# Attention scores of a head pair from 64 array rows each, in a PSUM bank each, with forget bias and mask added on VectorE

## The chip, the core and the metric

The program runs on one NeuronCore of a Trainium2 chip. Five engines work side by side, each through its own queue in order: TensorE (PE, matmuls into PSUM, with PEld for its weight loads), VectorE (DVE), ScalarE (ACT), GpSimd (POOL) and SyncE (SP), which here issues the weight loads. The metric is the device time of one execution in microseconds (us), the median of several runs.

## The reference

Two layers of a macaron block on 256 tokens of width 1024. The change lies in the forgetting attention of 8 heads of width 64; everything else (two SwiGLU blocks, a convolution branch, gates, a final gate) stays.

```
c  = cumsum(log_sigmoid(f_logit))                       # per head, over the tokens
for blk in 0, 1:                                        # blocks of 128 queries; keys up to the block's end
    sc = q[blk] @ k[:end].T * scale                     # (128 queries, 128 or 256 keys), contracted over 64
    sc = sc + (c[query] - c[key])                       # forget bias
    sc = where(query >= key, sc, -inf)
    pr = softmax(sc)
    out[blk] = pr @ v[:end]
```

In a softmax over the keys c[query] is the same for a whole row and drops out; only -c[key] matters.

## The kernel before, in words

Activations are kept transposed (`hT`, 128 features by 256 tokens per chunk). Each projection is done as three single-pass matmuls of split operands: `hi` and `lo` parts of the weights (`whi` made on ACT, `wlo` on DVE, lines 402 to 419) against `hi` and `lo` parts of the activations. Scores, transposes and probabilities times values stay plain fp32 matmuls, which the profile shows as two records each.

The order on PE, DVE and ACT is decided when the program is built. `Flow` (line 114) keeps a clock per engine; work is written as generators that yield (engine, planned cost, function) and waits on events or slots. `product` (line 258) puts the large projections on PE one after another, and lets the small operations of the generators in between whenever their planned time has come. DVE and ACT take the ready operation with the lowest `prio`; weight splits are fillers (`Weights.prio`, line 372), and the taps of the convolution (`taps`, line 919) have priority 4, so they fill what DVE has left. On the chip each engine then runs its list strictly in that order and waits where an input is late.

In `mixer` (line 898) the pieces that matter here follow one another on PE: the projections for the convolution and the values, the queries and keys (`heads`, line 1052), four gate blocks of 48 matmuls (line 1168), two blocks of 24 for `w_attn_out` (line 1191), two of 24 for `w_conv_out` (line 1217). The attention of four head pairs (`attention(j)`, line 1106) is slipped in between the gate matmuls.

Queries and keys lie in `QA` and `KA` with 66 rows per head: 64 features, and two rows that make the matmul add the forget bias (a row of ones against `ncum`, the negated running sum, and `cum` against ones). Each bank that `heads` fills holds four heads, the odd ones on partitions 64 to 127, so `heads_out` (line 1065) copies it in two halves to partitions 0 to 63. The 32 bias rows of both layers come by small DMAs from `forget` (line 994, DMAs at lines 1018 and 1019).

`softmax` (line 1079) runs once per pair and query block: two score matmuls into one bank of `xps` (two banks in all), a third matmul that adds the mask (`identb` against `later`, 256 columns of bf16), one DVE maximum over both heads, then per head an exponential on ACT that reads PSUM and sums, a reciprocal, and a scaling on ACT. Afterwards `attention` transposes the probabilities and multiplies by the values, each head into its own 64 partitions of one bank (line 1142).

The convolution ends with `conv_end` (line 1030): after the last tap ACT squares `acc` into `csq`, DVE adds it up, and PE sums over partitions (`xps<-ones,csq`). The chain goes on to `cs`, which the `w_conv_out` matmuls need.

Of the kernel before, what the change touches and what calls it, by code (L numbers as in the profile page):

```python
# [8 lines left out]
F32 = mybir.dt.float32  # L9
F32R = mybir.dt.float32r  # L10
I32 = mybir.dt.int32
BF16 = mybir.dt.bfloat16
AF = mybir.ActivationFunctionType
ALU = mybir.AluOpType
AX = mybir.AxisListType
PSUM = bass.MemoryType.PSUM

P = 128
T = 256
TT = T // P  # L20
D = 1024
KD = D // P
L = 2
H = 8
DH = 64
AW = H * DH
CC = 512
KC = CC // P
# [11 lines left out]
NEG = -3.0e38  # L40
# [19 lines left out]
PE, V, A = "pe", "vector", "scalar"  # L60


def vc(n, ptr=0):

    return 68 + 1.04 * n + 61 * ptr
# [6 lines left out]
class Event:  # L72
    at = None
# [10 lines left out]
class Slots:  # L84
# [6 lines left out]
    def ready(self):  # L91
        n = self.given - self.cap
        return 0 if n < 0 else self.ends.get(n)

    def take(self):
        self.given += 1
        return Handle(self, self.given - 1, self.make())


class Op:  # L100
# [13 lines left out]
class Flow:  # L114
# [9 lines left out]
    def spawn(self, gen, at=None, prio=1, lat=LAT):  # L124
        self.seq += 1
        c = Chain(gen, prio, lat, self.seq)
        self.resume(c, self.t[PE] if at is None else at, None)
        return c.ev
# [308 lines left out]
def trunk(ctx: ExitStack, tc: tile.TileContext, x, p, g_ff1, w_ff1_in, w_ff1_out, g_mix, w_in, b_f,  # L437
          w_attn_out, conv_w, conv_b, g_conv, w_conv_out, w_out, g_ff2, w_ff2_in, w_ff2_out,
          g_ple, w_ple_gate, w_ple_proj, g_final, out):
    nc = tc.nc  # L440
    tensor, vector, scalar = (Pinned(tc, e) for e in (nc.tensor, nc.vector, nc.scalar))
    flow = Flow()
    spawn, product = flow.spawn, flow.product
    pool = lambda **k: ctx.enter_context(tc.tile_pool(**k))
    const = pool(name="const", bufs=1)
# [5 lines left out]
    work = pool(name="work", bufs=2)  # L451
    small = pool(name="small", bufs=2)
    ps_mm = pool(name="ps_mm", bufs=6, space=PSUM)
    ps_x = pool(name="ps_x", bufs=2, space=PSUM)
    su_cm = tc.tile_pool(name="setup", bufs=1)
    su = su_cm.__enter__()
# [5 lines left out]
    xps = slots(2, ps_x, [P, 512], "xps")  # L462
# [3 lines left out]

    ident = const.tile([P, P], F32, name="ident")
    make_identity(nc, ident)

    identb = const.tile([P, P], BF16, name="identb")  # L470
    nc.gpsimd.tensor_copy(out=identb, in_=ident)
    later = const.tile([P, P], BF16, name="later")
    nc.gpsimd.memset(later, 0.0)
    nc.gpsimd.affine_select(out=later, in_=later, pattern=[[-1, P]], compare_op=ALU.is_ge, fill=NEG, base=0, channel_multiplier=1)
    ones = const.tile([P, P], F32, name="ones")
    vector.memset(ones, 1.0)
    by_token = const.tile([P, LINE], F32, name="by_token")
# [103 lines left out]
    def chunks(bank):  # L581
        return bank.t.rearrange("p (m t) -> p m t", m=2)
# [103 lines left out]
    class Norm:  # L686
        split_sum = False

        def __init__(self, gname, l):
            self.gname, self.l = gname, l  # L690
            self.xs = self.sum = self.got = None
            self.ready = [Event() for _ in range(KD)]
            self.tok, self.all, self.summed = Event(), Event(), Event()
# [114 lines left out]
    def bc(r, n, rows=P):  # L808
        return r.unsqueeze(1).to_broadcast([rows, n, T])
# [88 lines left out]
    def mixer(l, norm, nxt):  # L898
        W = w_in[l]
        norm.root()  # L900
        with tc.tile_pool(name="mixer", bufs=1) as ph, tc.tile_pool(name="attn", bufs=2) as at:
            QA = ph.tile([DH + 2, H, T], F32, name="QA")
            KA = ph.tile([DH + 2, H, T], F32, name="KA")
            abuf = ph.tile([P, KC, TAPS - 1 + T], F32, name="abuf")
            nc.gpsimd.memset(QA[DH:DH + 2], 1.0)
            nc.gpsimd.memset(KA[DH:DH + 2], 1.0)
            nc.gpsimd.memset(abuf[:, :, :TAPS - 1], 0.0)
            acc = ph.tile([P, KC, T], F32, name="acc")
            t1s, t2s = slots(2, at, [P, 512], "t1"), slots(2, at, [P, 512], "t2")
# [54 lines left out]
            in0 = spawn(conv_in(banks, (0, 1)))  # L964
# [29 lines left out]
            def forget():  # L994
                fl = at.tile([H, T], F32, name="fl", bufs=1)
                fe = at.tile([H, T], F32, name="fe", bufs=1)
                ncum = at.tile([H, T], F32, name="fc", bufs=1)
                bf = bf_t[:, l:l + 1]
                yield have_f8
                xp = yield xps  # L1000

                def go():
                    for tt in range(TT):
                        tensor.transpose(out=xp.t[:H, tt * P:(tt + 1) * P], in_=f8[:, tt], identity=ident)
                yield PE, 215, go

                yield A, ac(T), lambda: scalar.activation(out=fe, in_=xp.t[:H, :T], func=AF.Abs, bias=bf)
                yield A, ac(T) + 1283, lambda: scalar.activation(out=fe, in_=fe, func=AF.Exp, scale=-1.0)
                yield [(A, ac(T) + 1283, lambda: scalar.activation(out=fe, in_=fe, func=AF.Ln, bias=1.0)),
                       (V, vc(T), lambda: vector.tensor_scalar(out=fl, in0=xp.t[:H, :T], scalar1=bf, scalar2=0.0, op0=ALU.add, op1=ALU.min))]  # L1010
                xp.free()
                yield V, vc(T), lambda: vector.tensor_tensor(out=fl, in0=fl, in1=fe, op=ALU.subtract)
                cum = at.tile([H, T], F32, name="fe", bufs=1)
                oneb = ones[:H, 0:1].to_broadcast([H, T])
                yield V, vc(T), lambda: vector.tensor_tensor_scan(out=cum, data0=oneb, data1=fl, initial=0.0, op0=ALU.mult, op1=ALU.add)
                yield A, ac(T), lambda: scalar.activation(out=ncum, in_=cum, func=AF.Copy, scale=-1.0)
                for h in range(H):
                    nc.gpsimd.dma_start(out=QA[DH:DH + 1, h, :], in_=cum[h:h + 1, :])
                    nc.gpsimd.dma_start(out=KA[DH + 1:DH + 2, h, :], in_=ncum[h:h + 1, :])
                have_f.at = flow.now + 8000  # L1020
            spawn(forget(), prio=2)

            banks = block_a(W, norm.xs, KD, (C0 + 2 * P, C0 + CC + 2 * P), norm.ready)
# [28 lines left out]
            def heads(c0, dst, scale):  # L1052
                evs = []
                for mm in range(AW // (2 * P)):
                    bank = flow.take(mms)
                    blk = wts.take(W, 0, KD, c0 + mm * 2 * P, 2 * P)
                    for m in range(2):
                        for h in blk.halves:
                            ks = range(h.a, h.b)
                            piece(mm_b, MB, items_b(blk, bank, m, 0, ks, KD, norm.xs), [norm.ready[k] for k in ks])  # L1060
                    wts.release(blk)
                    evs.append(spawn(heads_out(bank, dst[:DH, 4 * mm:4 * mm + 4], scale)))
                return evs

            def heads_out(bank, dst, scale):
                yield norm.all
                for odd in range(2):
                    part, rows = dst[:, odd::2], slice(odd * DH, (odd + 1) * DH)
                    yield V, vc(2 * T), lambda: vector.scalar_tensor_tensor(out=part, in0=chunks(bank)[rows], scalar=scale,
                                                                            in1=bc(norm.rall[rows], 2, DH), op0=ALU.mult, op1=ALU.mult)  # L1070
                bank.free()

            have_qk = heads(Q0, QA, DH ** -0.5) + heads(K0, KA, 1.0)
# [2 lines left out]
            sms = slots(2, at, [P, TT, 2], "sm")  # L1076
            pTs = slots(1, at, [P, 6 * P], "pT")

            def softmax(h0, qb, sch, sm):

                sc, kl = sch.t, (qb + 1) * P
                xp = yield xps
                pt = xp.t.rearrange("p (h k) -> p h k", h=2)

                def go():
                    for i in range(2):
                        tensor.matmul(out=pt[:, i, :kl], lhsT=QA[:, h0 + i, qb * P:(qb + 1) * P], rhs=KA[:, h0 + i, :kl],
                                      start=i == 0, stop=False)
                    tensor.matmul(out=pt[:, :, qb * P:kl], lhsT=identb, rhs=later.unsqueeze(1).to_broadcast([P, 2, P]), start=False, stop=True)
                yield PE, 110 + 430 * (qb + 1), go  # L1090
                nm = small.tile([P, 2], F32, name=f"nm{qb}")
                yield V, vc(2 * kl), lambda: vector.tensor_reduce(out=nm, in_=pt[:, :, :kl], axis=AX.X, op=ALU.max, negate=True)

                def exps():
                    for i in range(2):
                        scalar.activation(out=sc[:, i], in_=pt[:, i, :kl], func=AF.Exp, bias=nm[:, i:i + 1], accum_out=sm[:, qb, i:i + 1])
                yield A, 2 * (ac(kl, 1) + 60), exps
                xp.free()
                yield V, vc(2), lambda: vector.reciprocal(out=sm[:, qb], in_=sm[:, qb])

                def norms():
                    for i in range(2):
                        scalar.activation(out=sc[:, i], in_=sc[:, i], func=AF.Copy, scale=sm[:, qb, i:i + 1])
                yield A, 2 * ac(kl, 1), norms

            def attention(j):
# [7 lines left out]
                    h = yield scs[qb]  # L1114
                    sch.append(h)
                sm = yield sms
                evs = [spawn(softmax(h0, qb, sch[qb], sm.t), at=flow.now) for qb in range(TT)]
                for e in evs:
                    yield e
                exp_done[j].at = flow.now  # L1120
# [289 lines left out]
```

## Time and profile before

| | |
|---|---|
| median of three runs | 1128.93 us (1128.48 to 1129.02) |
| profiled execution, device time | 1128.9 us |
| its span, first to last instruction | 1126.9 us |
| busy: PE, DVE, ACT, POOL | 1113.1, 833.3, 600.2, 30.5 us |
| granted TensorE clock | 0.998 of full speed |

The span is what the profile's instructions cover; about 2 us lie around it. A time "at 252.16" is counted from the span's start. A matmul's duration includes its way through the array and overlaps the next one's, so the cost of a matmul is read from start to start. Both layers run the same program; what layer 0 does at 252 us, layer 1 does at 804.7 us.

### The profile page before, as it was taken

How to read it: one execution, taken by the hardware profiler on the slowest of the kernel's cores; microseconds unless marked ns; L12 is line 12 of the kernel's file. 1: busy time of each engine (PE TensorE's matmuls, PEld its weight loads, DVE VectorE, ACT ScalarE, POOL GpSimd, SP SyncE). 2: the span in 40 equal slices, each digit the busy share in tenths (PEclk: the TensorE clock that was granted, in tenths of full speed). 3: DMA queues.
4: the chain of work that ended last, by engine and by line, in shares of the span. 5: the costliest groups of instructions: out<-in, count | busy, mean ns of one | idle time of the engine just before them, and what ended most of it. 6: DMA issues, size and time to landing. Idle time of an engine off the chain costs nothing.

```text
span 1126.9 us, 21344 instructions
## 1 busy us (share of the span) xinstructions
PE 1113.1 (99%) x8916; PEld 1069.8 (95%) x8916; DVE 833.3 (74%) x1256; ACT 600.2 (53%) x874; POOL 30.5 (3%) x58
## 2 busy tenths in 40 slices
PE   8999999999999999999999999999999999999997
PEld 8999999897789999999999999999877999999996
DVE  7766666899986867656896665569999787675665
ACT  6544445648555544444654444456566555444454
POOL 2000001020000000000000000012000000000000
PEclk9999999999999999999999999999999999999999
DMA  9655566454547565566466555664534656655541
GB/s 307 223 187 187 176 199 190 148 188 133 167 153 244 193 206 187 174 206 200 146 205 230 187 179 187 197 196 143 187 113 152 213 191 221 205 183 185 194 150 39
DMA packets 189665, 207.70 MB, mean 184 GB/s; under 512 B 5000, under 2 KB 174048, under 8 KB 189568
## 3 DMA queue, kind: packets, MB, share of 16 engines
q1 hardware_dynamic: 188064, 205.60, 55.7%
q8 instruction: 70, 1.15, 0.4%
q0 software_dynamic: 1472, 0.72, 0.3%
q14 instruction: 27, 0.22, 0.1%
q10 hardware_dynamic: 32, 0.01, 0.0%
HBM read 205.23 MB, written 1.05 MB: 183 GB/s over the span
## 4 chain that ended last, share of the span: by engine, by line
PE 81%; DVE 16%; ACT 2%; DMA 1%; issue 1%; SPq 0%; DVEq 0%; ACTq 0%
PE mmps L289 73%; PE xps L289 8%; DVE acc L289 8%; DVE wlo L289 5%; ACT sc L289 1%; DMA xin<-in_x_dram 1%; DVE nm L289 1%; DVE KA L289 0%; DVE QA L289 0%; ACT whi L289 0%; SPq L366 0%; DVE xs L289 0%; DVE csq L289 0%; ACT sq L289 0%; DVE sgate L289 0%
## 5 line engine op out<-in xcount | busy, mean ns | idle before, releaser
L289 DVE TENSOR_TENSOR wlo<-raw,whi 128x1024 fp32r<-128x1024 f32 (+3 forms) x400 | 471.5, 1191 | 200.2 <-ACT whi L289 153.4
L289 PE MATMUL mmps<-xs,whi 128*128 128x256 f32 x3456 | 593.3, 277 | 0.0
L289 ACT CAST whi<-raw 128x1024 fp32r<-128x1024 f32 (+3 forms) x400 | 405.2, 1023 | 342.0 <-PE mmps L289 282.0
L289 PEld LDWEIGHTS mmps<-xs,whi 128*128 128x128 f32 x3456 | 521.5, 188 | 0.6
L289 PE MATMUL mmps<-xs,wlo 128*128 128x256 f32 x1728 | 477.6, 276 | 0.0
L289 PEld LDWEIGHTS mmps<-xs,wlo 128*128 128x128 f32 x1728 | 324.4, 188 | 0.0
L289 PE MATMUL mmps<-whi,xs 128*128 128x512 f32 (+2 forms) x640 | 193.5, 377 | 0.0
L289 PE MATMUL mmps<-gs,whi 128*128 128x256 f32 x1056 | 179.7, 276 | 0.0
L289 PEld LDWEIGHTS mmps<-gs,whi 128*128 128x128 f32 x1056 | 158.9, 188 | 0.0
L289 PE MATMUL mmps<-gs,wlo 128*128 128x256 f32 x528 | 145.7, 276 | 0.0
L289 PEld LDWEIGHTS mmps<-whi,xs 128*128 128x128 f32 x640 | 116.1, 188 | 22.2 <-issue 1.4
L289 PE MATMUL mmps<-wlo,xs 128*128 128x512 f32 (+1 forms) x320 | 118.7, 371 | 0.0
L289 DVE SCALAR_TENSOR_TENSOR acc<-abuf,cols_taps,acc 128x256 f32<-128x256 f32 x240 | 100.5, 483 | 0.0
L289 PEld LDWEIGHTS mmps<-gs,wlo 128*128 128x128 f32 x528 | 99.1, 188 | 0.0
L289 PEld LDWEIGHTS mmps<-wlo,xs 128*128 128x128 f32 x320 | 60.3, 188 | 9.6
L289 PE MATMUL xps<-gs,whi 128*128 128x256 f32 x352 | 60.0, 276 | 0.0
L289 ACT CAST gs<-a 128x512 fp32r<-128x512 f32 x44 | 27.4, 623 | 53.2 <-DVE a L289 53.2
L289 PEld LDWEIGHTS xps<-gs,whi 128*128 128x128 f32 x352 | 52.9, 188 | 0.0
L289 PE MATMUL xps<-gs,wlo 128*128 128x256 f32 x176 | 48.6, 276 | 0.0
L289 ACT ACTIVATE xs<-hT,cols_mix 128x256 fp32r<-128x256 f32 (+1 forms) x56 | 28.2, 506 | 27.1 <-DVE hT L289 27.1
L289 DVE SCALAR_TENSOR_TENSOR hT<-mmps,hT 128x512 f32<-128x512 f32 x18 | 12.4, 691 | 32.6 <-PE mmps L289 32.5
L289 DVE TENSOR_TENSOR a<-a,mmps 128x512 f32<-128x512 f32 x44 | 30.3, 689 | 4.2
(143 smaller groups left out, 718.0 us busy)
## 6 DMA issues: line engine op xcount, KB each, us to landing
raw<-in_w_ff_in_dram SPq DMA_DIRECT2D x80, 1024.0 KB, 5.1
raw<-in_w_ff_out_dram SPq DMA_DIRECT2D x32, 896.0 KB, 4.9
raw<-in_w_in_dram SPq DMA_DIRECT2D x24, 1024.0 KB, 5.1
raw<-in_w_ff_out_dram SPq DMA_DIRECT2D x16, 1024.0 KB, 5.1
raw<-in_w_in_dram SPq DMA_DIRECT2D x16, 512.0 KB, 4.5
raw<-in_w_out_dram SPq DMA_DIRECT2D x16, 512.0 KB, 3.6
raw<-in_w_ple_gate_dram SPq DMA_DIRECT2D x8, 1024.0 KB, 5.1
raw<-in_w_ff_in_dram SPq DMA_DIRECT2D x12, 512.0 KB, 4.6
```

Of the source, the lines that this page charges most:

```text
L289: return self.tc.keep_in_program_order(f(*a, **k))
```

## The change

`QA` and `KA` become tiles of 128 partitions: the two heads of a pair stay where the projection put them, on partitions 0 to 63 and 64 to 127, and one DVE operation per bank copies both. The bias rows, the mask matmul and their setup on POOL go. `forget` writes `ncum` to a scratch tile in DRAM and reads it back to all 128 partitions (1 MB); POOL then makes `fb[0]` and `fb[1]` from it, the bias with the mask in it, with two `affine_select` operations. The score matmuls of one pair, both query blocks, are put on PE in one go, head 0 into one bank of `xps` and head 1 into the other; the pair waits for both banks (`Two`). Per head and query block one DVE `tensor_tensor_reduce` adds `fb` to the scores, negates, writes to SBUF and keeps the minimum (the negated maximum); ACT's exponential reads that SBUF tile.

```diff
+class Two(Slots):
+    def ready(self):
+        s = self.slots
+        ends = [s.ends.get(n) for n in (s.given - s.cap, s.given - s.cap + 1) if n >= 0]
+        return None if None in ends else max(ends, default=0)
+    def take(self):
+        return self.slots.take(), self.slots.take()
...
-    identb = const.tile([P, P], BF16, name="identb")
-    nc.gpsimd.tensor_copy(out=identb, in_=ident)
-    later = const.tile([P, P], BF16, name="later")
...
-            QA = ph.tile([DH + 2, H, T], F32, name="QA")
-            KA = ph.tile([DH + 2, H, T], F32, name="KA")
+            QA = ph.tile([P, KC, T], F32, name="QA")
+            KA = ph.tile([P, KC, T], F32, name="KA")
+            fb = [ph.tile([P, H, (qb + 1) * P], F32, name=f"fb{qb}") for qb in range(TT)]
-            nc.gpsimd.memset(QA[DH:DH + 2], 1.0)
-            nc.gpsimd.memset(KA[DH:DH + 2], 1.0)
...
-                for h in range(H):
-                    nc.gpsimd.dma_start(out=QA[DH:DH + 1, h, :], in_=cum[h:h + 1, :])
-                    nc.gpsimd.dma_start(out=KA[DH + 1:DH + 2, h, :], in_=ncum[h:h + 1, :])
-                have_f.at = flow.now + 8000
+                rows = drams.tile([H, T], F32, name="ncum")
+                nc.gpsimd.dma_start(out=rows, in_=ncum)
+                nc.gpsimd.dma_start(out=fb[1], in_=rows.partition_broadcast(P))
+                for dst, src in ((fb[0], fb[1][:, :, :P]), (fb[1][:, :, P:], fb[1][:, :, P:])):
+                    nc.gpsimd.affine_select(out=dst, in_=src, pattern=[[0, H], [-1, P]], compare_op=ALU.is_ge, fill=NEG, base=0,
+                                            channel_multiplier=1)
+                have_f.at = flow.now + 16000
...
             def heads_out(bank, dst, scale):
                 yield norm.all
-                for odd in range(2):
-                    part, rows = dst[:, odd::2], slice(odd * DH, (odd + 1) * DH)
-                    yield V, vc(2 * T), lambda: vector.scalar_tensor_tensor(out=part, in0=chunks(bank)[rows], scalar=scale,
-                                                                            in1=bc(norm.rall[rows], 2, DH), op0=ALU.mult, op1=ALU.mult)
+                yield V, vc(2 * T), lambda: vector.scalar_tensor_tensor(out=dst, in0=chunks(bank), scalar=scale, in1=bc(norm.rall, 2),
+                                                                        op0=ALU.mult, op1=ALU.mult)
...
-                evs = [spawn(softmax(h0, qb, sch[qb], sm.t), at=flow.now) for qb in range(TT)]
+                xp = yield Two(xps)
+                at_q = 0, P
+                def scores():
+                    for qb in range(TT):
+                        kl = (qb + 1) * P
+                        for i in range(2):
+                            rows = slice(i * DH, (i + 1) * DH)
+                            tensor.matmul(out=xp[i].t[:, at_q[qb]:at_q[qb] + kl], lhsT=QA[rows, j, qb * P:(qb + 1) * P], rhs=KA[rows, j, :kl],
+                                          start=True, stop=True)
+                yield PE, 850, scores
+                evs = []
+                for qb in range(TT):
+                    kl = (qb + 1) * P
+                    nm = small.tile([P, 2], F32, name=f"nm{qb}")
+                    def least():
+                        for i in range(2):
+                            vector.tensor_tensor_reduce(out=sch[qb].t[:, i], in0=xp[i].t[:, at_q[qb]:at_q[qb] + kl], in1=fb[qb][:, h0 + i],
+                                                        scale=-1.0, scalar=-NEG, op0=ALU.add, op1=ALU.min, accum_out=nm[:, i:i + 1])
+                    yield V, 2 * (vc(kl) + 80), least
+                    evs.append(spawn(softmax(qb, sch[qb].t, nm, sm.t), at=flow.now))
+                for x in xp:
+                    x.free()
```

In `softmax` the score and mask matmuls and the maximum are gone, and the exponential reads `sc` with scale -1 instead of PSUM.

The planned order moves with the planned costs. On PE, at the first head pair of layer 0 (`KA,QA` are the scores, `later,identb` the mask, `ident,sc` the transposes, `whi,xs` and `wlo,xs` the gate matmuls), before:

```order
L289 MATMUL mmps<-whi,xs 128x512
L289 MATMUL xps<-KA,QA 128x128 x2
L289 LDWEIGHTS identb
L289 MATMUL xps<-later,identb 128x2x128
L289 MATMUL xps<-KA,QA 128x256 x2
L289 LDWEIGHTS identb
L289 MATMUL xps<-later,identb 128x2x128
L289 MATMUL mmps<-whi,xs 128x512
```

and now:

```order
L304 MATMUL mmps<-wlo,xs 128x512
L304 MATMUL mmps<-whi,xs 128x512
L304 MATMUL xps<-KA,QA 128x128 x2
L304 MATMUL xps<-KA,QA 128x256 x2
L304 MATMUL mmps<-whi,xs 128x512
L304 MATMUL mmps<-wlo,xs 128x512
```

The two mask matmuls and their weight loads have left; the four score matmuls stand side by side, the two heads of a query block next to each other.

On PE at the end of the convolution (`ones,csq` is the sum of squares; with numbers, `xs_1830` is the normed input of the gates), before:

```order
L289 MATMUL mmps_3476<-wlo_3484,xs_1830 128x512
L289 MATMUL mmps_3476<-whi_3440,xs_1830 128x512
L289 MATMUL xps_3533<-ones_100,csq_3513 128x1 x2
L289 MATMUL mmps_3476<-whi_3444,xs_1830 128x512
L289 MATMUL mmps_3476<-wlo_3497,xs_1830 128x512
```

and now (`xs_1825` is the gates' input, `xs_2731` the attention's output, the operand of `w_attn_out`):

```order
L304 MATMUL mmps_3455<-wlo_3475,xs_1825 128x512
L304 MATMUL mmps_3455<-whi_3422,xs_1825 128x512
L304 MATMUL mmps_3546<-whi_3473,xs_2731 128x512
L304 MATMUL mmps_3546<-wlo_3509,xs_2731 128x512
L304 MATMUL mmps_3546<-whi_3473,xs_2731 128x512 x2
L304 MATMUL mmps_3546<-wlo_3509,xs_2731 128x512
L304 MATMUL mmps_3546<-whi_3473,xs_2731 128x512
L304 MATMUL xps_3543<-ones_95,csq_3531 128x1 x2
```

The sum of squares stood in the last gate block, behind 30 of its 48 matmuls; it now stands six matmuls into the first block of `w_attn_out`, with 294 matmuls of 512 columns of the layer ahead of it instead of 270. On DVE two more weight splits (91 instead of 89 of 1024 columns) stand ahead of its additions.

On DVE at the first head pair (`nm` is the negated maximum, an ISA row with `fb` the new reduction, the one after it the reading of its accumulator), before:

```order
L289 TENSOR_TENSOR wlo<-raw,whi 128x1024 x2
L289 SCALAR_TENSOR_TENSOR acc<-abuf,cols_taps_146,acc 128x256 x2
L289 TENSOR_REDUCE nm_3066<-xps 128x2
L289 SCALAR_TENSOR_TENSOR acc<-abuf,cols_taps_146,acc 128x256 x2
L289 TENSOR_REDUCE nm_3071<-xps 128x2
L289 RECIPROCAL sm<-sm 128x2
```

and now:

```order
L304 TENSOR_TENSOR wlo<-raw,whi 128x1024 x2
L304 SCALAR_TENSOR_TENSOR acc<-abuf,cols_taps_141,acc 128x256 x2
L304 ISA sc_3033,nm_3049<-xps,fb_2356 128x128
L304 ISA nm_3049 128x1
L304 ISA sc_3033,nm_3049<-xps,fb_2356 128x128
L304 ISA nm_3049 128x1
L304 ISA sc_3034,nm_3060<-xps,fb_2357 128x256
L304 ISA nm_3060 128x1
L304 ISA sc_3034,nm_3060<-xps,fb_2357 128x256
L304 ISA nm_3060 128x1
L304 RECIPROCAL sm<-sm 128x2
```

Two reductions have become eight instructions, with no tap between them.

## Rows read from the trace of the kernel before

**Rows 1.** Page: each engine's busy us, share of the span, instructions.

```profile
PE 1113.1 (99%) x8916; PEld 1069.8 (95%) x8916; DVE 833.3 (74%) x1256; ACT 600.2 (53%) x874; POOL 30.5 (3%) x58
```

**Rows 2.** Stretch of layer 0: us; busy PE, PEld, DVE, ACT, POOL; clock, DMA, GB/s.

```profile
225.00:301.00 76.00, 75.73 (x467) 64.31 (x467) 75.56 (x150) 46.10 (x96) 6.74 (x15) 1.00 0.48 154
```

**Rows 3.** Timeline of PE at the first head pair: start us, duration us, instruction.

```profile
251.93 0.39 PE L289 MATMUL mmps<-wlo,xs 128*128 128x512 f32 x1
252.16 0.39 PE L289 MATMUL mmps<-whi,xs 128*128 128x512 f32 x1
...
252.83 0.28 PE L289 MATMUL xps<-later,identb 128*128 128x256 bf16 x1
252.94 1.03 PE L289 MATMUL xps<-KA,QA 66*128 66x256 f32 x4
...
254.15 0.39 PE L289 MATMUL mmps<-wlo,xs 128*128 128x512 f32 x1
```

**Rows 4.** Timeline of PE at the third head pair.

```profile
261.62 0.39 PE L289 MATMUL mmps<-whi,xs 128*128 128x512 f32 x1
...
264.14 0.39 PE L289 MATMUL mmps<-wlo,xs 128*128 128x512 f32 x1
```

**Rows 5.** Timeline of PE at the first pair's probabilities times values.

```profile
265.08 0.40 PE L289 MATMUL mmps<-whi,xs 128*128 128x512 f32 x1
265.40 0.88 PE L289 MATMUL xps<-pT,v 128*64 128x256 f32 x8
...
266.56 0.40 PE L289 MATMUL mmps<-wlo,xs 128*128 128x512 f32 x1
```

**Rows 6.** Timeline of PE at the sum of squares of layer 0.

```profile
303.15 0.58 PE L289 MATMUL xps<-ones,csq 128*128 128x1 f32 x4 [1.00 <-DVE csq L289]
```

**Rows 7.** PE's waits: total us, times, longest.

```profile
PE xps L289 <- DVE csq L289: 2.0, 2, 1.0
```

**Rows 8.** Timeline of DVE: copies of the keys, weight splits, taps, maxima.

```profile
249.46 1.39 DVE L289 SCALAR_TENSOR_TENSOR KA<-mmps,rall 64x512 f32<-64x512 f32 x2
250.88 2.36 DVE L289 TENSOR_TENSOR wlo<-raw,whi 128x1024 fp32r<-128x1024 f32 x2
253.16 0.87 DVE L289 SCALAR_TENSOR_TENSOR acc<-abuf,cols_taps,acc 128x256 f32<-128x256 f32 x2
254.07 0.43 DVE L289 TENSOR_REDUCE nm<-xps 128x2 f32<-128x256 f32 x1
254.41 0.87 DVE L289 SCALAR_TENSOR_TENSOR acc<-abuf,cols_taps,acc 128x256 f32<-128x256 f32 x2
255.19 0.69 DVE L289 TENSOR_REDUCE nm<-xps 128x2 f32<-128x512 f32 x1
255.79 0.16 DVE L289 RECIPROCAL sm<-sm 128x2 f32<-128x2 f32 x1
255.87 0.86 DVE L289 SCALAR_TENSOR_TENSOR acc<-abuf,cols_taps,acc 128x256 f32<-128x256 f32 x2
```

**Rows 9.** Timeline of DVE at the running sum of the forget logits.

```profile
223.08 0.67 DVE L289 TENSOR_TENSOR_SCAN fe<-ones,fl 8x256 f32<-8x256 f32 x1
223.68 1.19 DVE L289 TENSOR_TENSOR wlo<-raw,whi 128x1024 fp32r<-128x1024 f32 x1
```

**Rows 10.** Timeline of POOL: a select of 128 elements, a fill of 2048, the first bias DMA.

```profile
1.12 0.29 POOL masks.py:199 TENSOR_SCALAR_AFFINE_SELECT ident<-ident 128x128 f32<-128x128 f32 x1
...
192.82 1.81 POOL L906 MEMSET KA<- 2x2048 f32 x1
...
224.04 0.50 POOL L1018 DMA_DIRECT2D QA<-fe  x1 [29.15 <-DVE fe L289]
```

**Rows 11.** Timeline of DVE while that fill runs.

```profile
192.94 1.24 DVE L289 TENSOR_TENSOR wlo<-raw,whi 128x1040 fp32r<-128x1040 f32 x1 [0.47 <-ACT whi L289]
```

**Rows 12.** DMA issues: count, KB each, median us from issue to landing.

```profile
raw<-in_w_in_dram SPq DMA_DIRECT2D x24, 1024.0 KB, 5.1
...
KA<-fc POOLq DMA_DIRECT2D x16, 1.0 KB, 4.0
```

More of the change, by code (lines that the diff above doesn't have):

```diff
@@ L97, in take, with __init__ @@
         return Handle(self, self.given - 1, self.make())
+class Two(Slots):
+    def __init__(self, slots):
+        self.slots = slots
+    def ready(self):
[4 more added lines that the diff above has]
+        return self.slots.take(), self.slots.take()
 class Op:
@@ L453, in trunk @@
     ps_mm = pool(name="ps_mm", bufs=6, space=PSUM)
+    drams = pool(name="drams", bufs=L, space=bass.MemoryType.DRAM)
     ps_x = pool(name="ps_x", bufs=2, space=PSUM)
@@ L468, in trunk @@
     make_identity(nc, ident)
-    identb = const.tile([P, P], BF16, name="identb")
-    nc.gpsimd.tensor_copy(out=identb, in_=ident)
-    later = const.tile([P, P], BF16, name="later")
-    nc.gpsimd.memset(later, 0.0)
-    nc.gpsimd.affine_select(out=later, in_=later, pattern=[[-1, P]], compare_op=ALU.is_ge, fill=NEG, base=0, channel_multiplier=1)
     ones = const.tile([P, P], F32, name="ones")
@@ L1061, in heads @@
                     wts.release(blk)
-                    evs.append(spawn(heads_out(bank, dst[:DH, 4 * mm:4 * mm + 4], scale)))
+                    evs.append(spawn(heads_out(bank, dst[:, 2 * mm:2 * mm + 2], scale)))
                 return evs
@@ L1077, in mixer, with softmax @@
             pTs = slots(1, at, [P, 6 * P], "pT")
[L1079 to L1092, printed above, removed]
+            def softmax(qb, sc, nm, sm):
+                kl = (qb + 1) * P
                 def exps():
                     for i in range(2):
-                        scalar.activation(out=sc[:, i], in_=pt[:, i, :kl], func=AF.Exp, bias=nm[:, i:i + 1], accum_out=sm[:, qb, i:i + 1])
+                        scalar.activation(out=sc[:, i], in_=sc[:, i], func=AF.Exp, scale=-1.0, bias=nm[:, i:i + 1], accum_out=sm[:, qb, i:i + 1])
                 yield A, 2 * (ac(kl, 1) + 60), exps
-                xp.free()
                 yield V, vc(2), lambda: vector.reciprocal(out=sm[:, qb], in_=sm[:, qb])
@@ L1116, in attention @@
                 sm = yield sms
-                evs = [spawn(softmax(h0, qb, sch[qb], sm.t), at=flow.now) for qb in range(TT)]
+                xp = yield Two(xps)
[10 more added lines that the diff above has]
+                for qb in range(TT):
+                    kl = (qb + 1) * P
+                    nm = small.tile([P, 2], F32, name=f"nm{qb}")
[7 more added lines that the diff above has]
+                    x.free()
                 for e in evs:
```

## The prediction

> **What bounds the kernel now.** I read the page's busy times first: PE works 1113.1 of the 1126.9 us of the span [rows 1], at full clock, so an edit can pay only by taking matmul time from PE or by shortening one of its few waits. Second, the stretch in which the change lies, 225 to 301 us of layer 0: here DVE is as full as PE, 75.56 of 76 us [rows 2]. DVE's list holds two kinds of work. Weight splits, copies and maxima are waited for soon; the taps of the convolution only have to be done before the sum of squares. So DVE's load shows at one place, where PE waits for that sum: 1.00 us in each layer, PE's longest waits for another engine behind the start [rows 6, 7]. PE would have gone on at 303.15 - 1.00 = 302.15 [rows 6]. Third, the timeline of PE around the scores, for the price of what goes.
>
> **What PE saves.** A 512-column matmul takes 0.23 us from start to start (251.93 to 252.16) [rows 3]. From the last gate matmul ahead of the first pair's scores to the second behind them pass 254.15 - 252.16 = 1.99 us; less two gate matmuls that is 1.53 us for four score and two mask matmuls [rows 3]. A mask matmul takes 0.11 us (252.83 to 252.94) [rows 3], so the scores alone take 1.53 - 0.22 = 1.31 us, one head after the other. The third pair, whose second block finds its bank still read, pays 264.14 - 261.62 - 0.46 = 2.06 us, 0.53 more [rows 4]; the second and fourth I count at 1.53.
> What two heads side by side cost, the trace shows for the other direction of the array: the probabilities times values write head 0 to partitions 0 to 63 and head 1 to 64 to 127, with the same 768 columns of fp32 as the scores, and take 266.56 - 265.08 - 0.46 = 1.02 us with all that entering and leaving costs [rows 5]. No row shows halves of the rows side by side. Bounds: 0.66 us (half of 1.31, no cost of entering) and 1.31 + 0.36 = 1.67 (nothing overlaps, but the 1.02 - 0.66 of entering and leaving is paid). I take 1.02, the nearest row. PE then saves 4 x (1.53 - 1.02) + 0.53 = 2.57 us per layer. That the pair now waits for both banks I cost at nothing: they come free when four reductions end, about 1.02 + 4 x 0.35 = 2.4 us after the scores begin, and twelve gate matmuls (2.8 us) stand between the first two pairs' scores, more between the others.
>
> **What DVE gains and loses up to the sum of squares, per layer.**
> Copies of queries and keys: two half copies take 250.88 - 249.46 = 1.42 us [rows 8]; one of 128x512 from PSUM takes 0.60, as the maximum over 512 columns does (255.19 to 255.79) [rows 8]. Four banks: 4 x 0.82 = 3.28 us less.
> Maxima: 0.34 (254.07 to 254.41) and 0.60 us per pair go [rows 8], 0.94. The reduction that comes is not in the trace. For 256 columns I take the maximum's 0.34 and for the reading of the accumulator 0.08, the shortest step on DVE (255.79 to 255.87) [rows 8]: 0.42. For 128 columns, at (0.60 - 0.34) / 256 = 1.0 ns per column, 0.21 + 0.08 = 0.29. A pair: 2 x (0.42 + 0.29) = 1.42; four pairs: 4 x (1.42 - 0.94) = 1.92 us more. Lower bound, with the readings free: 4 x (1.10 - 0.94) = 0.64. Upper bound from the only DVE row that carries a value along, the scan: 0.60 us for 256 columns (223.08 to 223.68) [rows 9], half of the columns' part for 128, 0.34, and 0.16 [rows 8] for each reading: 2 x (0.60 + 0.16 + 0.34 + 0.16) = 2.52 per pair, 6.3 us more.
> Weight splits: two more stand ahead of the sum, at (253.16 - 250.88) / 2 = 1.14 [rows 8]: 2.28 us. This is no new work, it is work done earlier.
> The selects on POOL: 1024 elements each. A select of 128 takes 0.29, a fill of 2048 1.81 us [rows 10], 0.84 ns for each further element: 0.29 + 896 x 0.84 ns = 1.04 us each; at most, if all grows with the elements, 8 x 0.29 = 2.32. They read SBUF, as taps and splits do with both inputs. No row shows POOL reading a tile while DVE works; while it only filled one, a split beside it kept its 1.24 us [rows 11]. So what they cost DVE lies between 0 and 4.64 us per layer. I take 2.08, both selects in full at the lower price: in a stretch where DVE has no gap, two engines on one memory are more likely to exclude each other than not to meet.
> The Trainium skill, "SBUF — State Buffer", section "Who interferes with whom", speaks against the change here: a DVE instruction with two SBUF inputs contends with a GpSimd one that reads SBUF, and the later one waits out the whole instruction of the earlier; against one that only writes it does not. The fill agrees with its second half [rows 11]. By the page DVE loses 2.08 us or more, without it nothing; these are the forecast and the first rival below.
> The bias in time: the first bias DMA leaves at 224.0 [rows 10]. The trip to DRAM takes 4.0 us as the bias rows do, the 1 MB back 5.1 like a weight block [rows 12], an issue of 0.5 us each [rows 10], then 2.1 to 4.6 for the selects: ready at 236 to 239, with 12 us in hand to the first reduction. Twice the DMA time would still do. Behind the waiting selects POOL has nothing to do until the next stage. The 1 MB shares the engines with weights, at a DMA share of 0.48 [rows 2], three blocks ahead: hidden. ACT's exponentials change their source only, with ACT idle for 30 of 76 us [rows 2].
>
> **The sum, per layer.** The sum was ready at 303.15. Now: 303.15 - 3.28 + 1.92 + 2.28 + 2.08 = 306.15. PE arrives there with 24 gate matmuls more in front: 302.15 - 2.57 + 24 x 0.23 = 305.10. So PE still waits, 1.05 us. Part of that it will pay earlier, at the first scores, when the keys are copied late; it is the same lateness and counts once. Set against the 303.15 + 24 x 0.23 = 308.67 at which it was as far before, PE gains 308.67 - 306.15 = 2.52 us. Behind the sum nothing is later than PE: in the kernel before PE needed `cs` about 16 us after the sum, now 5.5 us less, and the chain takes about 9 (estimates from the order's counts). Two layers: 5.0 us. The profiled execution took 1128.9 us, the median is 1128.93: 1128.9 - 5.0 = 1123.9.
>
> **Rivals.**
> *The selects cost DVE nothing.* For it: the split beside the fill [rows 11]. Against: a fill does not read. The sum is ready at 304.07, PE arrives at 305.10 and waits for nothing: 308.67 - 305.10 = 3.57 per layer, 1121.8.
> *The heads do not overlap* (the change does not do what it says). Rows of the array are not columns; the values' row is only a relative [rows 5]. PE's pair costs 1.67: 4 x (1.53 - 1.67) + 0.53, nothing saved. PE arrives at 302.15 + 5.52 = 307.67: 1.00 per layer, 1126.9.
> *The selects cost 2.32 each.* The sum is ready at 308.71: no gain, 1129.0.
> *The reduction is slow, and the kernel slower.* In place of the wait that shrinks, PE waits longer for the last tap. At the scan's pace [rows 9] DVE has 6.3 - 1.92 = 4.4 us more: the sum at 310.55, 1.9 lost per layer, 1132.7. It decides from 308.67 - 306.15 = 2.52 us per layer, a pair at more than 2.05 us in place of 1.42. Against: the maximum, a reduction too, runs at 1 ns per column [rows 8].
>
> **How the numbers follow.** Forecast 0.42, selects free 0.26, no overlap 0.12, dear selects 0.10, slow reduction 0.10. A measurement tells about 0.2% (2.3 us) from no change: faster is below 1126.7. The first two lie there, and of the third, whose 1.00 per layer is uncertain by as much, about half: 0.74. Same: the other half and the dear selects, 0.15; slower: the slow reduction and a little of the dear selects, 0.11. Range: the free selects with a cheaper pair at the lower end, 1120.7, the dear selects at the upper, 1128.9. The forecast's own range, 1122 to 1126, is that of the selects' price.
>
> **What would show it.** Score records of the two heads that start in pairs, and 1.0 us from gate to gate; the 128x512 copies 0.6 us apart; reduction and reading together 0.42 and 0.29; taps or splits that stretch, once per select, behind 234 us; PE's wait for `csq` near 1 us or, with an earlier one at the first scores, less. Wrong it would be if the scores wait for anything but the copies of the keys, if DVE waits for `fb`, or if PE's gain in the mixer is lost behind it, where PE has weights and `cs` to wait for.

## The result, and the profile after

| | before | changed |
|---|---|---|
| median | 1128.97 us (1128.48 to 1129.23, 4 runs) | 1121.98 us (1121.21 to 1122.48, 4 runs) |
| ratio | | 0.9936, 95% interval [0.9924, 0.9948] |
| span of the profiled execution | 1126.9 us | 1119.5 us |

The change makes the kernel 7.0 us faster; 5.0 were forecast, and the range, 1120.7 to 1128.9, holds the time. To see where the 7 us lie, count the matmuls that take `whi` or `wlo`: there are 8544 in both kernels. The stretch from the start of the 1951st to that of the 2201st encloses what changed in layer 0, the one from the 6231st to the 6481st the same in layer 1. Worked out from the start times in the traces:

| stretch | before | changed | difference |
|---|---|---|---|
| ahead, 25th to 1951st | 233.56 | 233.64 | +0.08 |
| layer 0, 1951st to 2201st | 71.31 | 67.57 | -3.73 |
| between, 2201st to 6231st | 482.11 | 482.11 | 0.00 |
| layer 1, 6231st to 6481st | 72.27 | 68.49 | -3.78 |
| behind, 6481st to the last | 243.80 | 243.80 | 0.00 |

Both layers give nearly the same, and nothing of size is given back elsewhere. The 25th of these matmuls begins between 12.0 and 12.8 us in the profiles of this study, whatever the kernel. Of a few tenths in a median, this start can be all; the stretches don't have it. The experiments below are compared by them.

Page of the changed kernel, each engine's busy time:

```profile
PE 1110.0 (99%) x8900; PEld 1065.2 (95%) x8900; DVE 830.3 (74%) x1296; ACT 600.4 (54%) x874; POOL 24.7 (2%) x27
```

PE is busy 3.1 us less than in [rows 1], and the span is 7.4 shorter. The difference of the busy times says too little here: in the first 12.6 us PE of this execution was busy 11.3 us, in that of before 9.6, and neither had got further by then. The table above is the safer reading. The stretch from 225 to 301 us (columns as in [rows 2]):

```profile
225.00:301.00 76.00, 76.00 (x471) 63.10 (x470) 74.94 (x169) 48.21 (x97) 8.38 (x4) 1.00 0.53 181
```

PE has no gap left. DVE, with 75.56 of 76 in [rows 2], now stands still for 1.06. The waits of PE, complete:

```profile
PE xps L304 <- ACT sq L304: 1.1, 1, 1.1
PE mmps L304 <- DVE eps L304: 1.1, 1, 1.1
PE mmps L304 <- DMA xin<-in_x_dram: 0.2, 1, 0.2
```

The wait for `csq` of [rows 7], twice 1.0, is no longer listed; what stands there lies at the start and the end of the kernel. PE around the scores of the first and of the third pair, which answers to [rows 3, 4]:

```profile
250.89 0.39 PE L304 MATMUL mmps<-whi,xs 128*128 128x512 f32 x1
251.21 0.93 PE L304 MATMUL xps<-KA,QA 64*128 64x128 f32 x8
252.07 0.50 PE L304 MATMUL mmps<-whi,xs 128*128 128x512 f32 x1
252.41 0.40 PE L304 MATMUL mmps<-wlo,xs 128*128 128x512 f32 x1
...
259.21 0.40 PE L304 MATMUL mmps<-whi,xs 128*128 128x512 f32 x1
...
260.73 0.40 PE L304 MATMUL mmps<-wlo,xs 128*128 128x512 f32 x1
```

By the measure of the prediction a pair takes 252.41 - 250.89 - 0.46 = 1.06 us, and so does the third, 260.73 - 259.21 - 0.46. Behind it, the sum of squares of layer 0, which answers to [rows 6]:

```profile
304.75 0.40 PE L304 MATMUL mmps<-whi,xs 128*128 128x512 f32 x1
305.05 0.58 PE L304 MATMUL xps<-ones,csq 128*128 128x1 f32 x4
305.49 0.48 PE L304 MATMUL mmps<-whi,xs 128*128 128x512 f32 x1
```

It begins 0.30 us after a matmul of `w_attn_out`, where such a matmul alone stands 0.23 behind the one before. DVE up to it (against [rows 8]): the second copy of keys, the reductions of the first pair, and the last two additions into `csq`:

```profile
249.93 0.68 DVE L304 SCALAR_TENSOR_TENSOR KA<-mmps,rall 128x512 f32<-128x512 f32 x1
250.53 2.35 DVE L304 TENSOR_TENSOR wlo<-raw,whi 128x1024 fp32r<-128x1024 f32 x2
...
253.59 0.28 DVE L304 CUSTOM_DVE_ANT_0 sc<-xps,fb 128x128 f32<-128x128 f32 x1
253.80 0.08 DVE L304 DVE_READ_ACCUMULATOR2_ANT nm<- 128x1 f32 x1
253.80 0.28 DVE L304 CUSTOM_DVE_ANT_0 sc<-xps,fb 128x128 f32<-128x128 f32 x1
...
254.01 0.42 DVE L304 CUSTOM_DVE_ANT_0 sc<-xps,fb 128x256 f32<-128x256 f32 x1
...
254.35 0.42 DVE L304 CUSTOM_DVE_ANT_0 sc<-xps,fb 128x256 f32<-128x256 f32 x1
254.70 0.08 DVE L304 DVE_READ_ACCUMULATOR2_ANT nm<- 128x1 f32 x1
...
303.76 1.15 DVE L304 TENSOR_TENSOR csq<-csq 128x512 f32<-128x512 f32 x2
```

The reading of the accumulator begins in the same moment as the next reduction and costs no time of its own: 0.21 us for 128 columns, 0.345 for 256, 1.11 for a pair. The additions end at 303.76 + 1.15 = 304.91, and PE could go on at 304.75 + 0.23 = 304.98. That looks like 0.07 us to spare, but it is not: PE begins at 305.05, 0.14 us behind the last addition. In the kernel before, where it waited in plain sight, it began 0.15 us behind it (303.15 [rows 6], and 301.85 + 1.15 = 303.00):

```profile
301.85 1.15 DVE L289 TENSOR_TENSOR csq<-csq 128x512 f32<-128x512 f32 x2
```

So PE still waits here, by a hair. Last, the two selects on POOL and DVE beside them:

```profile
233.26 5.63 POOL L1032 TENSOR_SCALAR_AFFINE_SELECT fb<-fb 128x1024 f32<-128x1024 f32 x1 [6.10 <-DMA fb<-ncum]
238.85 2.06 POOL L1032 TENSOR_SCALAR_AFFINE_SELECT fb<-fb 128x1024 f32<-128x1024 f32 x1
```

```profile
237.86 0.67 DVE L304 SCALAR_TENSOR_TENSOR QA<-mmps,rall 128x512 f32<-128x512 f32 x1
238.46 3.53 DVE L304 TENSOR_TENSOR wlo<-raw,whi 128x1024 fp32r<-128x1024 f32 x2
241.92 2.85 DVE L304 SCALAR_TENSOR_TENSOR acc<-abuf,cols_taps,acc 128x256 f32<-128x256 f32 x7
```

Two splits take 241.92 - 238.46 = 3.46 us, where two others take 252.80 - 250.53 = 2.27: 1.2 us lost. Read the ends together: the first select is ready at 233.26 and ends at 238.85, 0.99 us behind the start of a copy from PSUM (237.86). The six taps and two splits before that copy took their usual time. In layer 1 the first select ends 1.03 us behind the start of a copy too (787.65 for 786.62). So POOL waited 4.6 us for an instruction that does not read two tiles of SBUF, did its 1 us of work beside that copy, and ran 0.39 us into the split behind. The second select waited out that split, then held up the next.

### The profile page after: what moved, and what is told of

It is laid out like the page before. It is cut to its first block, busy times and chain, and to the rows that moved or that the text cites. A ratio compares the mean times of both kernels' runs of the same rounds, so it can differ in the third digit from the quotient of the medians.

```text
span 1119.5 us, 21305 instructions
## 1 busy us (share of the span) xinstructions
PE 1110.0 (99%) x8900; PEld 1065.2 (95%) x8900; DVE 830.3 (74%) x1296; ACT 600.4 (54%) x874; POOL 24.7 (2%) x27
## 3 DMA queue, kind: packets, MB, share of 16 engines
q8 instruction: 70, 1.15, 0.4%
HBM read 207.33 MB, written 1.06 MB: 186 GB/s over the span
## 4 chain that ended last, share of the span: by engine, by line
PE 98%; ACT 0%; DMA 0%; DVE 0%; issue 0%; SPq 0%; DVEq 0%; ACTq 0%
PE mmps L304 89%; PE xps L304 9%; DMA xin<-in_x_dram 0%; DVE sgate L304 0%; ACT sgate L304 0%; ACT sq L304 0%; DVE hT L304 0%; ACT L304 0%; SPq L381 0%; ACT xs L304 0%; DVE o L304 0%; DVEq L1430 0%; SPq L494 0%; DVE sqsum L304 0%; DVE rtok L304 0%
```

## The experiments

Each changes one thing in the changed kernel; the order of all instructions is otherwise as it was. "L0" and "L1" are the stretches of the first section, 67.57 and 68.49 us in the changed kernel; on another chip, in e8, 67.62 and 68.56.

| run | median | L0, L1 against the changed kernel |
|---|---|---|
| e1 scores head after head | 1121.61 (1120.92 to 1124.09) | -0.01, 0.00 |
| e6 both heads in one row half | 1126.25 (1125.65 to 1128.46) | +2.46, +2.49 |
| e7 large block first | 1121.96 (1121.29 to 1123.05) | -0.01, -0.01 (against e8) |
| e8 the changed kernel again | 1121.76 (1121.60 to 1122.50) | |
| e2 copies in halves | 1133.09 (1131.26 to 1133.30) | +3.97, +6.31 |
| e3 reductions twice | 1127.56 (1126.71 to 1129.24) | +2.85, +2.89 |
| e4 selects twice | 1124.97 (1124.70 to 1125.36) | +1.67, +1.71 |
| e5 fills for selects | 1120.86 (1120.57 to 1121.72) | -0.15, -0.13 |

**e1: what lets the heads overlap, their order?**

```diff
-for qb in range(TT):
-    kl = (qb + 1) * P
-    for i in range(2):
-        rows = slice(i * DH, (i + 1) * DH)
+for i in range(2):
+    rows = slice(i * DH, (i + 1) * DH)
+    for qb in range(TT):
+        kl = (qb + 1) * P
```

> The changed kernel, with a pair's scores issued head after head (head 0 for both query blocks, then head 1) and not block after block. Theory: two heads run beside each other only where their matmuls are neighbours in the order. Then only head 1's first block finds a neighbour (head 0's second), and a pair costs one 256-column matmul more, two passes of 0.215 = 0.43 us; 8 pairs: 3.4 us, 1125.4. DVE gains the same time, so PE still does not wait for the sum of squares. Rival: the order within the four does not matter, 1122.0.

The theory fell. PE at the first pair:

```profile
250.13 0.39 PE L304 MATMUL mmps<-whi,xs 128*128 128x512 f32 x1
250.45 0.93 PE L304 MATMUL xps<-KA,QA 64*128 64x128 f32 x8
251.31 0.50 PE L304 MATMUL mmps<-whi,xs 128*128 128x512 f32 x1
```

From gate to gate 251.31 - 250.13 = 1.18 us, as in the changed kernel (252.07 - 250.89). In the records of the single passes a second one begins 14 ns after the first, where it was 7. It can only be the other head's, as two passes of 128 columns in one half stand 0.11 us or more apart (e6), though both blocks of the first head stand ahead of it in PE's order.

**e6: or the halves of the rows?**

```diff
-rows = slice(i * DH, (i + 1) * DH)
+rows = slice(0, DH)
```

> The changed kernel, with the scores of both heads taken from the lower 64 rows (head 1's scores are then head 0's once more; all else, banks and order, as it was). Theory: only the other half of the rows lets the second head's matmuls run beside the first's, each half taking its own matmuls whatever stands ahead for the other. In one half they follow each other: 0.43 + 0.86 = 1.29 us in place of 0.65, 0.64 more per pair, 8 pairs: 5.1 us, 1127.0, which is the time of the rival without overlap. Rival A: the banks make the overlap, not the rows: 1121.8. Rival B: a small tile costs more to enter each time: above 1128.

```profile
250.47 0.39 PE L304 MATMUL mmps<-whi,xs 128*128 128x512 f32 x1
250.79 1.57 PE L304 MATMUL xps<-KA,QA 64*128 64x128 f32 x8
252.30 0.50 PE L304 MATMUL mmps<-whi,xs 128*128 128x512 f32 x1
252.64 0.39 PE L304 MATMUL mmps<-wlo,xs 128*128 128x512 f32 x1
```

252.30 - 250.47 = 1.83 in place of 1.18: 0.65 us per pair, as the theory had it. Four pairs are 2.60 us, and the layer is 2.46 to 2.49 longer: DVE has more time, and the 0.14 us that PE lost at the sum of squares goes. That the heads lie in different halves of the rows is worth all of the overlap; banks and order were the same here and gave none. The run also parts the gain of the change: the four pairs of layer 0 take 4 x 1.71 = 6.84 us here, no less than the 6.88 of the kernel before, and the layer is still 71.31 - 70.03 = 1.28 us shorter. That part comes from the wait at the sum of squares; what the mask matmuls and the late banks cost before, about 1.6 us per layer, entering and leaving the halves cost here.

**e7: what is the rest of a pair's time?** A pair takes 0.95 us where its columns alone would take 0.65.

```diff
-for qb in range(TT):
+for qb in reversed(range(TT)):
```

> The changed kernel, with the second query block's scores (256 columns) issued ahead of the first's (128). In the changed kernel the first pass behind a gate matmul takes 0.21 us from start to start where its 128 columns take 0.11 later on. Theory: what is paid there is the loading of the next weights, which a pass of 256 columns (0.215) covers; a pair then costs 0.1 us less, 8 pairs 0.8 us: 0.07% below the changed kernel on the same chip, 0.95 us per layer shown by the profile as 8 pairs of 0.85 in place of 0.95. Rival: the cost belongs to the change of the tile itself and is paid whatever comes first: no difference. The first reduction comes 0.1 to 0.3 us later after its scores, which DVE does not notice, as it is there more than 1 us later.

> The changed kernel as it is, on the same chip as the one beside it, for the comparison: 1121 to 1122.5. Both theories expect of it what it showed before.

The rival held. PE in e7 at the first pair:

```profile
250.94 0.39 PE L304 MATMUL mmps<-whi,xs 128*128 128x512 f32 x1
251.26 0.92 PE L304 MATMUL xps<-KA,QA 64*128 64x256 f32 x8
252.11 0.50 PE L304 MATMUL mmps<-whi,xs 128*128 128x512 f32 x1
```

252.11 - 250.94 = 1.17 us from gate to gate, in e8 1.18. The first pass takes 0.1 us more in either order (0.32 us for 256 columns, where a later one takes 0.21), so entering costs the same whatever comes first.

**e2: the copies of queries and keys.**

```diff
-vector.scalar_tensor_tensor(out=dst, in0=chunks(bank), ...)
+for odd in range(2):
+    rows = slice(odd * DH, (odd + 1) * DH)
+    vector.scalar_tensor_tensor(out=dst[rows], in0=chunks(bank)[rows], ...)
```

> The changed kernel, with each copy of queries and keys made in two halves of 64 rows as before the change: 0.82 us more on DVE four times per layer, 3.28 us. Theory: DVE has no slack in the mixer (its last addition for the sum of squares ends 0.07 us before PE is there), so PE waits 2.3 to 3.2 us per layer more, the larger part at the first scores (the last key copy ends at 250.6 + 3.3 = 253.9, PE is there at 251.2), the rest at the sum: 1126.6 to 1128.4. Rival: the wait at the sum went because PE's order changed, and DVE has slack: 1122.0 to 1123.

Slower than forecast, and slower than the kernel before (ratio 1.0034, interval [1.0022, 1.0047]); part of that is the clock, see below. PE waits, but not where I said:

```profile
255.29 0.39 PE L304 MATMUL mmps<-whi,xs 128*128 128x512 f32 x1
258.04 1.26 PE L304 MATMUL xps<-KA,QA 64*128 64x128 f32 x8 [2.35 <-DVE nm L304]
259.23 0.50 PE L304 MATMUL mmps<-whi,xs 128*128 128x512 f32 x1
```

The first pair needs the first copy of keys only and is not late. The second pair waits for the banks of the first: their reductions stand in DVE's list behind the second copy of keys, two splits and two taps. As the banks come free one after the other, its first head begins alone, and the block takes 259.23 - 258.04 = 1.19 us in place of 0.86. From gate to gate that is 259.23 - 255.29 = 3.94 us for 1.18, so 2.76 lost; with 1.0 us (from start to start) at a late split ahead of that and 0.2 behind it, 0.15 of them at the sum of squares, layer 0 is 3.97 longer for 3.28 us of copies. Layer 1 has the same wait and loses 2.3 us more, for another reason; stretches behind the wait in layer 0, then in layer 1 (columns as in [rows 2]):

```profile
258.00:262.00 4.00, 3.96 (x23) 3.18 (x24) 3.95 (x17) 4.00 (x14) 0.00 (x0) 1.00 0.69 248
```

```profile
810.00:814.00 4.00, 3.52 (x12) 2.58 (x13) 3.96 (x19) 4.00 (x14) 0.00 (x0) 0.56 0.74 260
814.00:818.00 4.00, 4.00 (x15) 3.28 (x14) 2.40 (x10) 2.86 (x12) 0.00 (x0) 0.58 0.26 36
```

Behind the wait in layer 1 the granted clock is 0.56 and 0.58 of full speed, so at the lower of its two levels, 1.2 GHz, for most of 8 us; behind the same wait in layer 0 it stays at 1.00.

**e3: the reductions.**

```diff
-for i in range(2):
+for i in (0, 1, 0, 1):
     vector.tensor_tensor_reduce(...)
```

> The changed kernel, with each of the new reductions run twice over the same data (16 + 16 more per layer, at 0.21 and 0.345 us a step with the reading inside: 4.4 us more on DVE per layer). Theory without slack on DVE: 3.5 to 4.4 us per layer at the sum of squares, 1129.0 to 1130.8, as the rival of the slow reduction had it. Rival with slack: 1122 to 1124.

DVE has 4.44 us more per layer, PE loses 2.85 to 2.89: neither all nor nothing. The waits of PE:

```profile
PE xps L304 <- DVE nm L304: 2.6, 6, 0.5
...
PE xps L304 <- DVE csq L304: 0.8, 2, 0.4
```

Most is lost at the banks again: in layer 0, from start to start, 0.9 us at the second pair's scores, 0.1 at the third's, and 0.5 and 0.4 at probabilities times values, which take a bank of `xps` too; the sum of squares adds 0.5. Another 0.4 at the last probabilities times values has no line among these waits. Of the 1.6 us that PE does not lose, 1.06 fall into times at which DVE of the changed kernel stood still: up to its last addition it is idle for 1.09 us in layer 0 there and for 0.03 here. The rest is open. With a pair's reductions at 2.22 us the kernel still beats the one before (ratio 0.9988, interval [0.9979, 0.9997]).

**e4: the selects.**

```diff
-for dst, src in ((fb[0], ...), (fb[1][:, :, P:], ...)):
+for dst, src in 2 * ((fb[0], ...), (fb[1][:, :, P:], ...)):
```

> The changed kernel, with both selects run twice (the same result). Theory: a select and a DVE instruction with two SBUF inputs exclude each other as whole instructions; a select gets in beside a copy from PSUM and holds up what follows. The second pair then costs DVE 1.2 us per layer like the first, paid at the first scores (0.7, the last key copy comes later) and at the sum: 2.4 us, 1124.3. Rival A: each select costs its whole 1.04: 2.1 per layer, 1126.1. Rival B: the longer splits have another cause: 1122.0.

Between the theory and rival A. The third and fourth select met no copy from PSUM; each held up one tap:

```profile
241.71 1.31 DVE L304 SCALAR_TENSOR_TENSOR acc<-abuf,cols_taps,acc 128x256 f32<-128x256 f32 x1
```

A tap takes 0.40 us from start to start, this one 1.23 (to 242.94): 0.83 lost, and as much at the next. POOL and DVE take turns here, one whole instruction each. DVE is 1.66 us later, and the layers are 1.67 and 1.71 longer: all of it comes back as PE's time. The place is the second pair's banks once more:

```profile
255.95 1.26 PE L304 MATMUL xps<-KA,QA 64*128 64x128 f32 x8 [1.05 <-DVE nm L304]
```

**e5: POOL that only writes.**

```diff
-nc.gpsimd.affine_select(out=dst, in_=src, ...)
+nc.gpsimd.memset(dst, 0.0)
```

> The changed kernel, with a fill of zeros in place of each select (POOL writes the same elements and reads none; forget bias and mask are left out). Theory: a fill holds up no DVE instruction, so both splits behind 238.5 take 1.13 us again and DVE is 1.2 us earlier in each layer; PE waits for neither the banks nor the sum in the changed kernel, so the time stays, 1121.5 to 1122. Rival A: any work of POOL holds DVE up, the splits stay long. Rival B: PE still pays for DVE's lateness somewhere, and 1.2 us per layer come back: 1119.5.

```profile
237.87 2.34 DVE L304 TENSOR_TENSOR wlo<-raw,whi 128x1024 fp32r<-128x1024 f32 x2
240.14 0.47 DVE L304 SCALAR_TENSOR_TENSOR acc<-abuf,cols_taps,acc 128x256 f32<-128x256 f32 x1
```

Two splits take 2.27 us again, 1.2 less than in the changed kernel, also those beside the second fill (0.96 us at 232.77; the first needs no bias and runs at 190.7). Of these 1.2 us DVE has 0.6 left at the last addition (57.97 us behind the 1951st matmul, in the changed kernel 58.59), as 0.4 go into waits for scores and exponentials. PE gains only what it still lost at the sum of squares, 0.13 to 0.15 us per layer. The median is lower by more than that, 1.1 us; of this the profile shows 0.5 in the start (12.15 us to the 25th matmul, 12.69 in the changed kernel), where no select has run. So without the selects there is almost nothing to win, and with twice as many their whole cost is PE's: the changed kernel stands at the edge. None of the runs points to a faster kernel.

## Why the prediction was right, and where not

**PE's saving: right.** A pair at 1.06 us where 1.02 was taken from the values; entering and leaving cost the two directions of the array alike. The four pairs of layer 0 took 6.88 us and take 4.24: 2.64 us per layer (2.57 forecast). Two errors cancel: pairs cost 0.04 more, and the second pair before, counted at 1.53, took 1.73 in two pieces, as the records of its passes show. The rival without overlap had 1.67 for a pair; e6 builds that case: 252.64, the second gate matmul behind, less 250.47 and 0.46 is 1.71, and the time is within 0.7 us of the one named (1126.25 for 1126.9).

**"So PE still waits, 1.05 us": wrong, and the step that failed.** PE begins the sum of squares 0.07 us later than it could (305.05 for 304.98). The mechanism was right, PE and DVE racing to that point; three terms of DVE's sum were off. Against the 303.15 of the kernel before:

| term per layer | forecast | measured, layer 0 |
|---|---|---|
| copies, 4 x (0.60 - 1.42) | -3.28 | -3.28 |
| two weight splits earlier | +2.28 | +2.27 |
| reductions in place of maxima | +1.92 | 4 x (1.11 - 0.94) = +0.68 |
| selects | +2.08 | +1.2 |
| DVE standing still | 0 | 1.06 - 0.13 = +0.93 |

The reductions were over-priced because I added a reading of 0.08 to each; the lower bound in the prediction, readings free, was the right row of reasoning. The selects came to 1 us each, as taken, but one of them found a copy from PSUM to run beside. The 0.84 ns per element behind them does not come out of [rows 10], which give (1.81 - 0.29) / 1920 = 0.79; little hangs on it. And a term was missing: DVE now gets ahead of ACT's exponentials. Its longest waits for `sc` in the changed kernel are these; with the shorter ones they are 1.06 us up to the last addition, before they were 0.13:

```profile
260.28 0.17 DVE L304 RECIPROCAL sm<-sm 128x2 f32<-128x2 f32 x1 [0.35 <-ACT sc L304]
...
262.81 0.17 DVE L304 RECIPROCAL sm<-sm 128x2 f32<-128x2 f32 x1 [0.48 <-ACT sc L304]
```

The measured terms add to +1.80. The last addition ends at 304.91, against 303.00 before, 1.91 later; 0.11 of that is the start of this execution (the 1951st matmul begins at 246.32, before at 246.21). So the terms account for the shift.

The price of the wait before was misread as well. Its 1.00 us is idle time behind a matmul's duration of 0.39; from start to start the matmul takes 0.23. PE before, and in e5, where DVE is in time:

```profile
301.75 0.40 PE L289 MATMUL mmps<-whi,xs 128*128 128x512 f32 x1
...
303.59 0.47 PE L289 MATMUL mmps<-whi,xs 128*128 128x512 f32 x1
```

```profile
304.17 0.39 PE L304 MATMUL mmps<-whi,xs 128*128 128x512 f32 x1
304.40 0.50 PE L304 MATMUL xps<-ones,csq 128*128 128x1 f32 x4
304.77 0.48 PE L304 MATMUL mmps<-whi,xs 128*128 128x512 f32 x1
```

With the sum of squares between them the two matmuls lie 0.60 us apart in e5, 1.84 before and 305.49 - 304.75 = 0.74 in the changed kernel. So the wait cost 1.24 and costs 0.14. The layer gains 3.73 us instead of 2.52: 2.64 at the scores, 1.10 here (they add to within the rounding), where the forecast had 2.57 and a wait 0.05 longer than before.

**The time of the first rival, not its reason.** 1121.8 was named for selects that cost nothing. They cost 1.2 us; the cheaper reductions, 1.2 us below the forecast, made up for it. That 1121.98 falls on this rival's time, at the edge of the forecast's own range of 1122 to 1126, is luck. The Trainium skill, "SBUF — State Buffer", section "Who interferes with whom", says of two SBUF inputs against a GpSimd instruction that reads, that the later waits out the earlier. The traces agree: turns of whole instructions in e4, no stretch beside a fill in e5 and none of the copy from PSUM. The first select went beyond it, as it waited out eight instructions, not one. What the rule alone does not give is the bill, as that hangs on which instruction DVE has next.

**"That the pair now waits for both banks I cost at nothing": right by a hair, and by the wrong reckoning.** I let the reductions follow the scores at once and had 2.4 us against 2.8. In fact the reductions stand in DVE's list, start 2.4 us after the scores (253.59 against 251.21), and the last reading ends at 254.78, 0.26 us ahead of the second pair (255.04). About 0.2 of that is slack: in e2, where it waits, PE begins the pair 0.06 us behind the reading that frees the first bank (258.04 behind 257.98). That is where lateness of DVE shows first in e3 and e4, and most in e2, not at the sum of squares. Had the selects and reductions cost what I took, PE would have waited there too; e4, 1.66 us later, says by about as much as DVE was late.

**The bias: in time, as forecast.** DMA issues of the changed kernel (columns as in [rows 12]):

```profile
fb<-ncum POOLq DMA_DIRECT2D x2, 1024.0 KB, 6.7
...
ncum<-fc POOLq DMA_DIRECT2D x2, 8.0 KB, 1.6
```

The way to DRAM was shorter than taken (4.0), the way back longer (5.1). The second select ends at 238.85 + 2.06 = 240.91, later than the 236 to 239 I had, as the first waited; the first reduction comes 12.7 us later.

**The slow reduction.** It was to decide from 2.05 us a pair. e3, at 2.22 with the same selects, is 1.2 us faster than before: the selects were cheaper and the wait dearer than reckoned, which moved the point, and a third of DVE's extra time did not reach PE.

## What to carry to other kernels

Where one engine is full and another nearly so, look for every place at which the first waits on the second's list, and write down the slack at each: here none at one, where PE still loses 0.14 us, and about 0.2 at the other; the other, costed at nothing, is the one that charges first when DVE is later still (e3, e4). Compare the distance between the two engines with a run that plainly waits: by the end times alone the first place seemed to have 0.07 us to spare. A price of a new instruction that is a sum of two (a reduction and its reading) is to be kept as a range until a trace shows whether they overlap. And when a change lands this close to the edge, test it from both sides, with the cost doubled and with the cost gone.

## What the runs showed of the hardware

- Two matmuls in different halves of the rows run beside each other even when others stand between them in program order (e1: second head 14 ns after the first, 7 when neighbours; the block takes 1.18 us from gate to gate either way); in the same half they follow each other (e6: 1.83 us for 1.18).
- A select on POOL that reads SBUF, 1 us of work, took 5.6 us while DVE ran splits and taps without a gap, 4.6 of them waiting; once it ran, the two took turns (e4: taps of 0.40 us became 1.23).
- Reading the accumulator behind a reduction starts together with the next reduction and costs no step on DVE (both begin at 253.80; 0.21 us a step for 128 columns).
- PE begins 0.14 to 0.15 us behind the last DVE addition that it waits for (303.15 behind 303.00 before, 305.05 behind 304.91 now).
- After PE's wait of 2.35 us the granted clock fell to 0.56 and 0.58 in the 8 us behind in one layer, so for the most part to the lower level of 1.2 GHz, and stayed at 1.00 in the other, in the same execution (e2).
